# A hybrid decoder layer on one core: own buffers for the second recurrence's preparation, five weight-buffer pairs and a lag of two in the mixers, and the exclusive decay read as a shift

## The chip, the core and the metric

The kernel runs on one core of a Trainium2 chip. The metric is the device time of one execution in microseconds (us), lower is better. PE is the matrix engine (TensorE), DVE the vector engine, ACT the scalar engine, POOL is GpSimd, and SP issues most of the DMAs. The diff to be judged touches only the middle third of the program, and the memory pools around it.

## The reference, cut to what matters

A layer of width 2048 over 256 tokens, with three residual stages, all in float32:

```python
x = layer_norm(alpha * x + 0.5 * swiglu(x, ffn1...))             # d_ff 5632
p = x @ w_in                                                       # 3*1024 + 3*1024 + 288 columns
o_attn = diff_attn_group(p[..., :3072], ...)                       # 8 heads, causal
o_rwkv = rwkv7_group(p[..., 3072:], ...)                           # 16 heads of 64, a delta-rule recurrence
x = layer_norm(alpha * x + concat([o_attn, o_rwkv]) @ w_out)
x = layer_norm(alpha * x + 0.5 * swiglu(x, ffn2...))

# in rwkv7_group, per head and per token t (state is 64 x 64):
state = state * w_t + (state @ -kk_t) x (kk_t * a_t) + v_t x k_t   # w_t = decay, kk = normalised k
y_t   = state @ r_t
# afterwards: group norm of y, plus a bonus term, times a gate g
```

Inside a chunk of 64 tokens the kernel needs the running product of the decays up to and including a token (it multiplies r), and the product up to but *excluding* it (it multiplies kk). It keeps logarithms, so the first is exp of a running sum, and the second exp of that sum less the token's own term.

## The kernel before, in words

**Main matmuls.** Each weight matrix streams through SBUF in steps: SP loads two 128-row slices of 512 columns (`raw`, L127), ACT rounds them to `wh` (L130), and DVE subtracts to get the rest, `wl` (L131). Activations are split likewise into `xh` and `xl` (L80, L81). A product is three matmuls, hi*hi, lo*hi and hi*lo (L107, L108, L109), so a step is 12 main matmuls: 6 for token half tt=0 and 6 for tt=1. There are 664 steps and 7968 main matmuls. `stream.block` (L113) runs one block of 512 columns over its row slices. tt=1's half of a step is issued `LAG` = 4 steps behind tt=0's, and a ring of `NW` = 7 pairs `wh`, `wl` holds the weights.

**Program order.** All in-between work (recurrence, attention heads) is written as Python generators. After each step `run_bg` (L142) lets them write instructions up to a budget of credit. The engines then run their instructions in the order in which a list scheduler put them; every engine is a strict queue. The order is fixed before the run.

**The stages.** ffn1; LayerNorm 1 (L178 to L192); the mixers; LayerNorm 2 (the same lines); ffn2; LayerNorm 3. In the mixers the blocks of `w_in` come as: the 288-column lora block (8 steps), then k, r, v of recurrence group 1 (8 heads), v, k, q of attention group 1, and the same for group 2, 12 blocks of 8 steps (96 main matmuls). Then `w_out` runs in three parts of its rows: part (0,2) needs attention group 1 and recurrence group 1, part (1,) attention group 2, part (3,) recurrence group 2. Its partial sums stay in SBUF as `y` (written at L868, added to at L870).

**A recurrence group** (`rwkv_group`, L470). The *preparation*: lora matmuls and sigmoids (L485 to L490), running sum (L495), a subtract and three Exp (L497, L498, L500, L501), normalising kk (L507 to L521), products with the decays, the matrix `Q` of all chunks (L558, L561). Then a triangular *solve* as 62 short DVE operations (L581, L583) in a layout that a DMA makes and DMAs undo (L587, L588, L595, L599). Then the *chain*, the part that runs along the chunks (L606 to L680), and the group norm and gate (L693 to L728), which end in `og`, rows of `w_out`'s operand. Both groups use the same tiles `AR`, `BKc`, `vv`, `Q` and the scratch tiles T1, T2 and lw; group 2's generator is held until group 1's chain has been written (L472), and the writes of its r, k, v until group 1 has done with the tiles (L412, L420). All small products of both groups go through one PSUM pool, `sm`, with three banks, handed out in program order.

**The y buffers.** Of part (0,2)'s four column blocks two lie in tiles that the attention of group 2 still reads (`k` and an `H5` tile that holds v), so their L868 must wait for that.

## Time and profile before

| | us |
|---|---|
| runs | 2008.81, 2011.87, 2012.96; median 2011.87 |
| the profiled execution | 2011.4 |
| its span in the profile | 2009.6 |
| PE busy in the span | 1964.6 (98%) |
| PE's weight loads (PEld) | 1614.0 (80%) |
| DVE busy | 1148.2 (57%) |
| ACT busy | 888.1 (44%) |

The span runs from the first to the last instruction; the profiled execution's own time is 1.8 us longer. A row of the trace's timeline has a start, a duration, an engine, the line, the operation and its tiles, and in brackets how long the engine had been idle just before and who released it. Matmuls are pipelined, so durations of neighbours overlap: what one costs is the distance between starts. The granted clock (PEclk) is TensorE's clock as a share of 2.4 GHz.

### The profile page before, as it was taken

What the parts mean: (1) busy time and instruction counts of PE and PEld (TensorE: products, weight loads), DVE (VectorE), ACT (ScalarE), POOL (GpSimd) and SP (SyncE); (2) the same over time, 40 slices, a digit from 0 to 9 for tenths busy, and PEclk for the clock granted to TensorE, in tenths of its full rate; (3) what the DMA queues carried; (4) which work ended last, traced back from release to release, by engine and by line L of the source; (5) the groups of instructions that cost most, each with busy time, mean ns of one, the idle gap of its engine ahead of it and who ended that gap; (6) DMA issues with size and microseconds to landing.
All of it is one profiled execution on the core that took longest, in us unless ns stands there. A gap on an engine that the chain in (4) does not pass through costs nothing. (4 is left out here: it accounts for less than half of the span.)

```text
span 2009.6 us, 24928 instructions
## 1 busy us (share of the span) xinstructions
PE 1964.6 (98%) x9671; PEld 1614.0 (80%) x9671; DVE 1148.2 (57%) x1420; ACT 888.1 (44%) x1100; POOL 34.3 (2%) x68
## 2 busy tenths in 40 slices
PE   8999999999999999999999988999999999999997
PEld 7888888888888878887777767788888888888886
DVE  5555454445545566776667766745555444554555
ACT  5444443344444336645574444444444334444432
POOL 0200000000000000000000000000000000000000
PEclk9999999999999999999999979999999999999999
DMA  7766666667666656656535625666666666766663
GB/s 238 216 188 191 187 193 207 208 197 230 189 189 188 194 178 194 178 158 175 145 86 169 203 70 169 202 201 188 191 187 192 207 210 195 230 190 188 190 195 128
DMA packets 202008, 373.35 MB, mean 186 GB/s; under 512 B 22826, under 2 KB 24944, under 8 KB 201120
## 3 DMA queue, kind: packets, MB, share of 16 engines
q1 hardware_dynamic: 182928, 350.53, 58.2%
q10 hardware_dynamic: 17440, 14.29, 2.5%
q0 software_dynamic: 1520, 6.93, 1.1%
q8 instruction: 76, 1.25, 0.3%
q14 instruction: 44, 0.36, 0.1%
HBM read 364.10 MB, written 7.60 MB: 185 GB/s over the span
## 5 line engine op out<-in xcount | busy, mean ns | idle before, releaser
L131 DVE TENSOR_TENSOR wl<-raw,wh 128x1024 fp32r<-128x1024 f32 (+1 forms) x665 | 807.8, 1216 | 655.6 <-ACT wh L130 654.3
L130 ACT CAST wh<-raw 128x1024 fp32r<-128x1024 f32 (+1 forms) x665 | 695.8, 1047 | 840.6 <-PE acc L109 711.3
L109 PE MATMUL acc<-wh,xl 128*128 128x512 f32 (+1 forms) x1952 | 739.7, 390 | 1.5 <-DVE xl L81 1.5
L108 PE MATMUL acc<-wl,xh 128*128 128x512 f32 (+1 forms) x1952 | 736.3, 392 | 0.9 <-DVE wl L131 0.9
L107 PE MATMUL acc<-wh,xh 128*128 128x512 f32 (+1 forms) x1952 | 724.5, 391 | 9.4 <-ACT xh L80 7.5
L107 PEld LDWEIGHTS acc<-wh,xh 128*128 128x128 f32 x1952 | 367.4, 188 | 88.7 <-ACT xh L80 9.0
L108 PEld LDWEIGHTS acc<-wl,xh 128*128 128x128 f32 x1952 | 367.6, 188 | 77.0 <-issue 2.0
L109 PEld LDWEIGHTS acc<-wh,xl 128*128 128x128 f32 x1952 | 367.5, 188 | 75.9 <-DVE xl L81 2.0
L109 PE MATMUL acc<-wh,hh 128*128 128x512 f32 x704 | 254.4, 390 | 0.0
L108 PE MATMUL acc<-wl,hh 128*128 128x512 f32 x704 | 253.5, 389 | 0.0
L107 PE MATMUL acc<-wh,hh 128*128 128x512 f32 x704 | 252.7, 389 | 0.0
L108 PEld LDWEIGHTS acc<-wl,hh 128*128 128x128 f32 x704 | 132.2, 188 | 27.6
L109 PEld LDWEIGHTS acc<-wh,hh 128*128 128x128 f32 x704 | 132.2, 188 | 27.3
L107 PEld LDWEIGHTS acc<-wh,hh 128*128 128x128 f32 x704 | 132.1, 188 | 27.3
L234 DVE TENSOR_TENSOR hh<-tr,hh 128x512 fp32r<-128x512 f32 x44 | 30.4, 691 | 64.0 <-ACT hh L233 64.0
L233 ACT CAST hh<-tr 128x512 fp32r<-128x512 f32 x44 | 25.8, 587 | 91.0 <-PE tr L223 91.0
L220 DVE SCALAR_TENSOR_TENSOR h<-sg,acc 128x512 f32<-128x512 f32 x44 | 30.2, 687 | 34.9 <-PE acc L109 34.8
L215 ACT ACTIVATE sg<-acc 128x512 f32<-128x512 f32 x44 | 26.4, 600 | 43.6 <-PE acc L109 43.5
L581 DVE TENSOR_TENSOR itmp<-U,Y 64x31 f32<-64x31 f32 (+15 forms) x62 | 20.5, 331 | 11.5 <-DMA U<-dU 10.2
L223 PEld LDWEIGHTS tr<-ident,h 128*128 128x128 f32 x176 | 21.8, 139 | 5.7
L223 PE MATMUL tr<-ident,h 128*128 128x128 f32 x176 | 26.3, 271 | 0.0
L583 DVE TENSOR_TENSOR Y<-Y,itmp 64x31 f32<-64x31 f32 (+15 forms) x62 | 20.6, 332 | 1.4
(247 smaller groups left out, 750.8 us busy)
## 6 DMA issues: line engine op xcount, KB each, us to landing
raw<-in_ffn_w_up_dram SPq DMA_DIRECT2D x176, 512.0 KB, 3.9
raw<-in_ffn_w_down_dram SPq DMA_DIRECT2D x176, 512.0 KB, 4.2
raw<-in_ffn_w_gate_dram SPq DMA_DIRECT2D x175, 512.0 KB, 3.9
raw<-in_w_in_dram SPq DMA_DIRECT2D x96, 512.0 KB, 3.9
raw<-in_w_out_dram SPq DMA_DIRECT2D x32, 512.0 KB, 4.5
rc<-xs ACTq DMA_DIRECT2D x16, 256.0 KB, 4.3
lng<-in_ln_g_dram POOLq DMA_DIRECT2D x3, 1024.0 KB, 7.9
lnb<-in_ln_b_dram POOLq DMA_DIRECT2D x3, 1024.0 KB, 9.7
```

The costliest lines, as they stand in the source:

```text
L107: T.matmul(a, hi, wh[:, j, :w], start=(ki + j == 0), stop=False)
L108: T.matmul(a, hi, wl[:, j, :w], start=False, stop=False)
L109: T.matmul(a, lo, wh[:, j, :w], start=False, stop=(ki + j == last))
L130: SC.copy(out=wh[:, c, :w], in_=raw[:, c, :w])
L131: V.tensor_tensor(out=wl[:, c, :w], in0=raw[:, c, :w], in1=wh[:, c, :w].bitcast(F32), op=ALU.subtract)
L215: SC.activation(out=s, in_=acc, func=AF.Silu)
L220: V.scalar_tensor_tensor(out=h, in0=sg[tt], scalar=0.5, in1=acc, op0=ALU.mult, op1=ALU.mult)
L223: T.transpose(tr[:, i, :], h[:, i * P:(i + 1) * P], ident)
L233: SC.copy(out=hi, in_=tr)
L234: V.tensor_tensor(out=lo, in0=tr, in1=hi.bitcast(F32), op=ALU.subtract)
L581: V.tensor_tensor(out=tv, in0=U[:, 0:j, j:j + 1].to_broadcast([64, j, 32 - j]), in1=Y[:, j:j + 1, j:32].to_broadcast([64, j, 32 - j]), op= ...
L583: V.tensor_tensor(out=Y[:, 0:j, j:32], in0=Y[:, 0:j, j:32], in1=tv, op=ALU.add)
```

## The change

- **Buffers.** A class `Group` gives the second recurrence its own `AR`, `BK`, `vv` (tags ARd, BKd, vvd) and its own scratch (`tl`; `cum` lies in a half of `qq`). The two holds (L472 before, and the `until` calls in `done`) go; one hold is left, ahead of `Q`. The gate weights g2 no longer lie in `Q`.
- **Room for it.** In the mixers the ring has five pairs and the lag is two; in the two ffn stages seven and four as before. Two of the seven pairs lie in a pool of each stage.
- **Decay.** L497 and L498 go: the exclusive product at a token is the inclusive one of the token before it in the chunk, so `al[:, :, 1:64]` is multiplied by `cum[:, :, 0:63]`. The order of the preparation's products changes, and the first product of `be` and the copy `PC` move.
- **y and ln2.** `y` lies in group 1's old `AR` and `BK` memory (tags J0, BKc). LayerNorm 2's gain and bias, loaded by POOL, go to J1 and Q and are issued when part (3,) begins.
- **Credit.** Each generator has its own credit (`BG` 1.6, attention heads `AT` 0.5) in place of one shared budget.
- The scratch memory for DMA descriptors of GpSimd's queue is set to 2048.

```diff
-LAG = 4
-NW = 7
+LAG = {"ffn": 4, "mix": 2}
+NW = {"ffn": 7, "mix": 5}
...
-                wh = wp.tile([P, n, NB], F32R, tag="wh", name=nm("wh"), bufs=NW)
-                wl = wp.tile([P, n, NB], F32R, tag="wl", name=nm("wl"), bufs=NW)
+                pool = wp if self.slot < NW["mix"] else self.pool
+                wh, wl = (pool.tile([P, n, NB], F32R, tag=f"{t}{self.slot}", name=nm(t)) for t in ("wh", "wl"))
+                self.slot = (self.slot + 1) % NW[self.name]
...
-                if len(self.pend) > max(0, min(LAG, self.step // 4 - 1)):
+                if len(self.pend) > max(0, min(LAG[self.name], self.step // 4 - 1)):
...
-        AR = hp.tile([P, 4, 4, 2, 64], F32, tag="J0", name="AR")
-        BK = mp.tile([P, 4, 4, 3, 64], F32, tag="BKc", name="BKc")
-        vp = mp.tile([P, 4, 64 + S], F32, tag="vv", name="vv")
+        class Group:
+            def __init__(self, g):
+                self.AR = (hp, mp)[g].tile([P, 4, 4, 2, 64], F32, tag=("J0", "ARd")[g], name=nm("AR"))
+                self.BK = mp.tile([P, 4, 4, 3, 64], F32, tag=("BKc", "BKd")[g], name=nm("BK"))
+                self.vp = mp.tile([P, 4, 64 + S], F32, tag=("vv", "vvd")[g], name=nm("vv"))
...
-                    if prev is not None:
-                        stream.until(lambda: ("chain", "cols", "gate")[i] in prev)
...
-            prev = st["prev"]
-            while prev is not None and "chain" not in prev:
-                yield None
...
-            V.tensor_tensor(out=lw, in0=cum, in1=lw, op=ALU.subtract)
-            SC.activation(out=lw, in_=lw, func=AF.Exp, scale=-LDEC)
...
-            V.scalar_tensor_tensor(out=merge(al), in0=merge(al), scalar=-1.0, in1=merge(v4(lw)), op0=ALU.mult, op1=ALU.mult)
...
+            V.tensor_tensor(out=merge(al)[:, :, 1:64], in0=merge(al)[:, :, 1:64], in1=merge(v4(cum))[:, :, 0:63], op=ALU.mult)
...
-            while prev is not None and "end" not in prev:
+            while prev is not None and "chain" not in prev:
                 yield None
...
-        gb = load_gb(mp, A["ln2_g"], A["ln2_b"], "J0", "BKc")
+        gb = []
...
-                yt = [hp.tile([P, 2, NB], F32, tag="H3", name=nm("yt")), qq[:, 0].rearrange("p a s -> p (a s)").rearrange("p (t n) -> p t n", t=2),
-                      hp.tile([P, 2, NB], F32, tag=HT["k"], name=nm("yt"))]
-                yj = hp.tile([P, 2, NB], F32, tag="H5", name=nm("yv"))
+                yt = [hp.tile([P, 4, NB], F32, tag="J0", name=nm("y")), mp.tile([P, 4, NB], F32, tag="BKc", name=nm("y"))]
+                y = [[yt[n // 2][:, 2 * (n % 2) + t, :] for n in range(4)] for t in range(2)]
+            if 3 in qs:
+                gb.extend(load_gb(mp, A["ln2_g"], A["ln2_b"], "J1", "Q"))
...
-    nc = bacc.Bacc("TRN2", target_bir_lowering=False, num_devices=1)
+    nc = bacc.Bacc("TRN2", target_bir_lowering=False, num_devices=1, dynamic_dma_scratch_size=2048)
```

Where the instructions land, at three places. First, PE ahead of the second group's chain (acc is a main matmul's sum, YT the solve's transposed result, TT and PT blocks of the solve, ot an attention head's output). Before:

```order
4808 L108 MATMUL acc_9615<-wl_9667,xh_9144 128x512
4809 L109 MATMUL acc_9615<-wh_9666,xl_9145 128x512
4810 L109 MATMUL acc_9622<-wh_9586,xl_9149 128x512
4811 L107 MATMUL acc_9622<-wh_9586,xh_9148 128x512
4812 L108 MATMUL acc_9622<-wl_9587,xh_9148 128x512
4813 L109 MATMUL acc_9622<-wh_9586,xl_9149 128x512
4814 L606 MATMUL sm_8552<-YT_8548,Q 32x32 x32
4815 L617 MATMUL sm_8589<-TT_8542,PT_8549 32x32
4816 L627 MATMUL sm_8644<-ident,BKc 128x64 x8
4817 L825 MATMUL at_9343<-ident,ot_9279 128x128 x2
```

And now (lines have moved: L113 to L115 are the main matmuls, L608 was L606):

```order
4837 L115 MATMUL acc_9640<-wh_9629,xl_9150 128x512
4838 L113 MATMUL acc_9640<-wh_9668,xh_9149 128x512
4839 L114 MATMUL acc_9640<-wl_9669,xh_9149 128x512
4840 L115 MATMUL acc_9640<-wh_9668,xl_9150 128x512
4841 L113 MATMUL acc_9640<-wh_9668,xh_9149 128x512
4842 L114 MATMUL acc_9640<-wl_9669,xh_9149 128x512
4843 L608 MATMUL sm_8451<-YT_8447,Q 32x32 x32
4844 L115 MATMUL acc_9640<-wh_9668,xl_9150 128x512
4845 L619 MATMUL sm_8507<-TT_8441,PT_8448 32x32
4846 L629 MATMUL sm_8544<-ident,BK_7242 128x64 x8
4847 L829 MATMUL at_9414<-ident,ot_9319 128x128 x2
```

Counted over the whole order, 4542 main matmuls stand ahead of the first row of L606 before, and 4566 now: the 24 of part (0,2)'s last column block, tt=1, have moved ahead of the chain, and the first L825 of that head pair stood behind the chain's start and its counterpart now stands ahead of it.

Second, DVE where group 2's preparation starts (T, then qq, is the running sum; L708, L711, L713, later L711, L714, L716, finish group 1's norm). Before:

```order
696 L708 TENSOR_TENSOR BKc<-BKc,Q 128x16x64
697 L495 SCALAR_TENSOR_TENSOR T_1340_7273<-smask,lw_7252 128x256 x2
698 L711 TENSOR_SCALAR BKc<-BKc,vB 128x4x64 x4
699 L358 SCALAR_TENSOR_TENSOR AR<-praw_7845,om,df_7947 128x4x64
700 L524 TENSOR_SCALAR Q<-BKc,vB 128x256
701 L713 TENSOR_TENSOR Q<-BKc,vv 128x1024
702 L495 SCALAR_TENSOR_TENSOR T_1340_7273<-smask,lw_7252 128x256 x2
```

Now:

```order
692 L711 TENSOR_TENSOR BK_5614<-BK_5614 128x16x64
693 L714 TENSOR_SCALAR BK_5614<-BK_5614,vB 128x4x64 x4
694 L505 SCALAR_TENSOR_TENSOR qq<-smask,tl_7245 128x256
695 L138 TENSOR_TENSOR wl_8418<-raw_8416,wh_8417 128x1024
696 L716 TENSOR_TENSOR BK_5614<-BK_5614,vv_5615 128x16x64
697 L367 SCALAR_TENSOR_TENSOR AR_7241<-praw_7834,om,df_7923 128x4x64
698 L514 TENSOR_SCALAR BK_7242<-BK_7242,vB 128x4x64 x2
699 L505 SCALAR_TENSOR_TENSOR qq<-smask,tl_7245 128x256 x3
```

Group 2's running sum stands at the end of group 1's norm in both orders, beside the same weight step (the 352nd `wl`). It has not moved ahead of the first chain. Counted in main matmuls, group 2's lora product (L485, now L496) stands at 4117 before and 4129 now, its norm (L517, L519) at 4136 and 4175, and its `Q` (L558, L555) at 4237 to 4270 and 4257 to 4295; the solve begins beside `wl` 366 and 367 and ends beside `wl` 384 in both.

Third, ACT from the first LayerNorm 2 output to the first steps of ffn2 (at, sm: transposed columns; xs: the DMA that saves the normalised rows). Before:

```order
728 L192 DMA xs_83<-yt_9152 128x512
729 L80 CAST xh_10036<-at_10031 128x512
730 L192 DMA xs_83<-qq 128x512
731 L130 CAST wh_10231<-raw_10230 128x1024
732 L80 CAST xh_10048<-sm_10043 128x512
733 L192 DMA xs_83<-yt_9153 128x512
734 L80 CAST xh_10060<-at_10055 128x512
735 L130 CAST wh_10250<-raw_10249 128x1024
736 L192 DMA xs_83<-yv_9154 128x512
737 L80 CAST xh_10072<-sm_10067 128x512
738 L130 CAST wh_10268<-raw_10267 128x1024
```

Now:

```order
726 L201 DMA xs_83<-y_9154 128x512
727 L81 CAST xh_10073<-at_10068 128x512
728 L201 DMA xs_83<-y_9154 128x512
729 L81 CAST xh_10085<-sm_10080 128x512
730 L201 DMA xs_84<-y_9153 128x512 x2
731 L201 DMA xs_84<-y_9154 128x512 x2
732 L81 CAST xh_10126<-at_10121 128x512
733 L81 CAST xh_10138<-sm_10133 128x512
734 L81 CAST xh_10150<-at_10145 128x512
735 L81 CAST xh_10162<-sm_10157 128x512
736 L137 CAST wh_10248<-raw_10247 128x1024
737 L137 CAST wh_10266<-raw_10265 128x1024
```

The two casts of weights that stood between the first half's columns are gone from there: ffn2's sixth pair, `wh_10248`, has to wait for memory that the xs DMAs of the second half still read, and all four of those DMAs stand ahead of the second half's casts. In PE's order, 30 main matmuls of ffn2 now stand ahead of the second half's transposes, where about 44 stood; at the boundary from ffn1 to the mixers 30 of the 288-column matmuls, where 42 stood. Of `w_out`, 24 main matmuls follow the last one of the first token half (36 before), and 12 stand between the last transposes of part (1,) and the first that needs `og` (24 before).

## Rows read from the trace of the kernel before

**Rows 1.** The page: busy time by engine (its first part), and the chain that ended last, by engine.
```profile
PE 1964.6 (98%) x9671; PEld 1614.0 (80%) x9671; DVE 1148.2 (57%) x1420; ACT 888.1 (44%) x1100; POOL 34.3 (2%) x68
PE 37%; DVE 2%; ACT 1%; DMA 0%; issue 0%; DVEq 0%; ACTq 0%
```

**Rows 2.** Busy time by stretch: us from the span's start, length, then busy us (and instructions) of PE, PEld, DVE, ACT, POOL, the granted clock of PE, the DMA share, GB/s.
```profile
743.90:760.00 16.10, 12.64 (x93) 11.52 (x92) 15.61 (x27) 6.83 (x12) 0.99 (x1) 1.00 0.72 219
...
1040.00:1080.00 40.00, 37.91 (x201) 29.58 (x200) 33.38 (x43) 21.20 (x26) 0.00 (x0) 1.00 0.51 148
...
1150.00:1175.00 25.00, 17.52 (x245) 13.49 (x246) 14.48 (x39) 12.35 (x32) 2.01 (x2) 0.68 0.36 99
1175.00:1200.00 25.00, 21.70 (x259) 17.80 (x257) 17.99 (x56) 10.71 (x36) 2.01 (x2) 0.84 0.15 42
...
1250.00:1275.00 25.00, 21.52 (x101) 17.43 (x101) 24.86 (x38) 8.36 (x10) 2.00 (x2) 1.00 0.68 202
...
1300.00:1500.00 200.00, 200.00 (x902) 165.63 (x901) 102.11 (x92) 84.85 (x90) 0.30 (x2) 1.00 0.67 192
```

**Rows 3.** PE's timeline, main matmuls of 512 columns: the first and the last of thirteen in a row.
```profile
1146.05 0.39 PE L109 MATMUL acc<-wh,xl 128*128 128x512 f32 x1
...
1148.79 0.39 PE L109 MATMUL acc<-wh,xl 128*128 128x512 f32 x1
```

**Rows 4.** PE's timeline where ffn1 ends and the mixers' lora block begins: the first and the last of 39 matmuls of 288 columns in a row, and the second half's transposes that follow.
```profile
746.13 0.30 PE L107 MATMUL acc<-wh,xh 128*128 128x288 f32 x1
...
751.13 0.29 PE L109 MATMUL acc<-wh,xl 128*128 128x288 f32 x1
753.80 1.29 PE L74 MATMUL tr<-ident,y 128*128 128x128 f32 x8 [2.38 <-DVE y L187]
```

**Rows 5.** By source line: the subtract and the Exp of the exclusive decay (ns, minimum, median, maximum; first and last start).
```profile
L497 DVE TENSOR_TENSOR lw<-T,lw x2: 1217/1220/1224, 786.8 to 1036.2; 128x1024 f32<-128x1024 f32 x2
...
L498 ACT ACTIVATE lw<-lw x2: 1039/1043/1047, 789.5 to 1038.8; 128x1024 f32<-128x1024 f32 x2
```

**Rows 6.** Timelines of ACT and DVE in group 2's preparation: one table load, and DVE's longest wait there.
```profile
1040.78 1.28 ACT L520 ACT_TABLE_LOAD   x1
...
1027.15 1.23 DVE L708 TENSOR_TENSOR BKc<-BKc,Q 128x1024 f32<-128x1024 f32 x1 [5.83 <-ACT Q L706]
```

**Rows 7.** Timelines of DVE, ACT's DMA issues and PE from the end of group 2's solve to the start of its chain.
```profile
1144.73 0.18 DVE L583 TENSOR_TENSOR Y<-Y,itmp 64x31 f32<-64x31 f32 x1
1144.95 1.12 DVE L586 COPY U<-Y 64x1024 f32<-64x1024 f32 x1
...
1146.11 0.34 ACTq L588 DMA_DIRECT2D dYT<-U  x1
...
1152.49 0.98 ACTq L599 DMA_DIRECT2D YT<-dYT  x2
...
1152.22 0.40 PE L109 MATMUL acc<-wh,xl 128*128 128x512 f32 x1
1154.94 0.24 PE L606 MATMUL sm<-YT,Q 32*32 32x32 f32 x2 [2.32 <-DMA YT<-dYT]
```

**Rows 8.** Timelines of DVE and PE in the chain: the first and the last of three writes of y, and the first main matmul after the chain's first three quarters.
```profile
1172.52 0.67 DVE L868 SCALAR_TENSOR_TENSOR yt<-rc,acc 128x512 f32<-128x512 f32 x1
...
1186.08 0.68 DVE L868 SCALAR_TENSOR_TENSOR yv<-rc,acc 128x512 f32<-128x512 f32 x1
...
1192.94 0.50 PE L107 MATMUL acc<-wh,xh 128*128 128x512 f32 x1 [0.82 <-ACT xh L80]
```

**Rows 9.** Busy time by stretch again (columns as in Rows 2): the three stretches at the low clock, and the boundary to ffn2.
```profile
1155.80:1169.40 13.60, 11.30 (x182) 8.96 (x176) 8.70 (x23) 7.83 (x18) 1.01 (x1) 0.50 0.37 119
1172.80:1183.10 10.30, 8.39 (x92) 7.22 (x94) 7.29 (x25) 5.57 (x24) 0.00 (x0) 0.50 0.19 53
1227.50:1234.30 6.80, 3.46 (x8) 2.82 (x9) 3.86 (x6) 1.14 (x2) 0.54 (x1) 0.50 0.43 154
1259.80:1279.00 19.20, 14.86 (x78) 11.58 (x76) 19.17 (x29) 6.60 (x10) 1.00 (x1) 1.00 0.85 255
```

**Rows 10.** Timelines of PE and DVE from group 2's last norm product to the first matmul on `og`.
```profile
1217.80 1.89 PE L703 MATMUL sm<-Q,bones 128*128 128x256 f32 x8
...
1228.85 1.28 DVE L728 TENSOR_TENSOR og<-Q,sm 128x512 f32<-128x512 f32 x2
...
1230.84 0.80 PE L107 MATMUL acc<-wh,xh 128*128 128x512 f32 x1 [5.96 <-ACT xh L80]
```

**Rows 11.** Timelines of DVE and PE at LayerNorm 2: the last sum of the first half, the last cast of the second, and PE's last long waits.
```profile
1252.50 0.67 DVE L870 TENSOR_TENSOR yv<-yv,acc 128x512 f32<-128x512 f32 x1
...
1280.00 0.68 DVE L81 TENSOR_TENSOR xl<-sm,xh 128x512 fp32r<-128x512 f32 x1
...
1264.42 0.63 PE L74 MATMUL sm<-ident,yv 128*128 128x128 f32 x4 [1.73 <-DVE yv L187]
1266.12 0.50 PE L109 MATMUL acc<-wh,xl 128*128 128x512 f32 x1 [1.07 <-DVE xl L81]
```

**Rows 12.** DMA issues between 1250 and 1285 us: count, KB of one, median us from issue to landing.
```profile
xs<-yt ACTq DMA_DIRECT2D x4, 256.0 KB, 4.8
xs<-qq ACTq DMA_DIRECT2D x2, 256.0 KB, 3.7
```

**Rows 13.** The page's fifth part: all of DVE's weight subtractions (busy us, mean ns).
```profile
L131 DVE TENSOR_TENSOR wl<-raw,wh 128x1024 fp32r<-128x1024 f32 (+1 forms) x665 | 807.8, 1216 | 655.6 <-ACT wh L130 654.3
```

More of the change, by code (lines that the diff above doesn't have):

```diff
@@ L141, in flush, with spawn, run_bg @@
                 self.mm(self.pend.pop(0), 1)
-        def run_bg(self, budget):
-            self.credit = min(self.credit, 0.0) + budget
-            idle = 0
-            while self.bg and self.credit > 0 and idle < len(self.bg):
-                g = self.bg.pop(0)
-                try:
-                    cost = next(g)
-                except StopIteration:
-                    continue
-                self.bg.append(g)
-                if cost is None:
-                    idle += 1
-                else:
-                    idle = 0
-                    self.credit -= cost
+        def spawn(self, gen, rate):
+            self.bg.append(gen)
+            self.credit[gen] = [0.0, rate]
+        def run_bg(self):
+            for g in list(self.bg):
+                c = self.credit[g]
+                c[0] = min(c[0], 0.0) + c[1]
+                while c[0] > 0 and g in self.bg:
+                    try:
+                        cost = next(g)
+                    except StopIteration:
+                        self.bg.remove(g)
+                        break
+                    if cost is None:
+                        break
+                    c[0] -= cost
         def until(self, ready):
@@ L406, in rwkv_cols @@
             st["gen"] = rwkv_group(g, st)
-            stream.bg.append(st["gen"])
+            stream.spawn(st["gen"], BG)
             def done(tt, acc, i):
                 if tt == 0:
-                    if i == 2 and prev is not None:
-                        stream.until(lambda: "chain" in prev)
-                    pr = hp.tile([P, 4, S + 1], F32, tag=("H3", "H3", "J1")[i], name=nm("praw"))
+                    pr = hp.tile([P, 4, S + 1], F32, tag="J1" if g == 0 and i == 2 else "H3", name=nm("praw"))
                     V.memset(pr[:, :, 0:1], 0.0)
@@ L446, in rwkv_values @@
         def rwkv_values(g, st):
-            rk = st["rk"]
+            prev = st["prev"]
+            while "rk" not in st or (prev is not None and "chain" not in prev):
+                yield None
+            vp, vv, rk = st["group"].vp, st["group"].vv, st["rk"]
             SV = hp.tile([P, 4, 4, 2, 64], F32, tag="J1", name=nm("SV"))
@@ L521, in rwkv_group @@
[L521 to L526 removed]
+            SC.activation(out=tl, in_=tl, func=AF.Ln)
+            SC.activation(out=tl, in_=tl, func=AF.Exp, scale=-0.5)
@@ L562, in rwkv_group @@
                 yield 1.2
+            rk = t4("lw")
+            for p in range(4):
+                V.scalar_tensor_tensor(out=v4(rk)[:, p], in0=rh[:, p], scalar=col(4, g, p), in1=ka[:, p], op0=ALU.mult, op1=ALU.mult)
+            st["rk"] = rk
+            yield 1.5
             dU = dp.tile([64, 32, 32], F32, tag="dU", name=nm("dU"))
@@ L712, in rwkv_group @@
             yield 0.6
-            V.tensor_tensor(out=v4(sq), in0=Yc, in1=v4(vv), op=ALU.add)
+            V.tensor_tensor(out=sq, in0=Yc, in1=v4(vv), op=ALU.add)
             yield 0.6
             st["gate"] = True
-            while g == 0 and "r" not in st.get("next", ()):
+            while g == 0 and "v" not in st.get("next", ()):
                 yield None
-            o = (hp, mp)[g].tile([P, 4, S], F32, tag=("H3", "vv")[g], name=nm("og"))
+            o = (hp, mp)[g].tile([P, 4, S], F32, tag=("H3", "vvd")[g], name=nm("og"))
             for hf in range(2):
```

128 lines of the change are left out of this document (62 added, 66 removed).

## The prediction

> **What bounds the kernel now.** I read the page first. PE is busy for 1964.6 of 2009.6 us, and the chain that ended last runs over PE and hardly anything else [rows 1]. So the only time to be had is where PE stands idle or runs slowly, and a cheaper DVE or ACT instruction is worth nothing by itself. Next I read the busy time by stretch [rows 2]: in 200 us of ffn2 PE has no gap, and what it loses in the middle lies in a few places. Between ffn1 and the mixers it loses 16.1 - 12.6 = 3.5 us. In group 2's preparation (1040 to 1080) it loses 40.0 - 37.9 = 2.1 us. Around group 2's chain (1150 to 1200) it loses 10.8 us, and part of the rest runs at the low clock. It waits 6.0 us for og [rows 10], and at LayerNorm 2 it loses 19.2 - 14.9 = 4.3 us [rows 9]. That, with the slow matmuls inside, is all that this change can move.
>
> The unit for all that follows is one main matmul: thirteen starts in a row span 1148.79 - 1146.05 = 2.74 us, so 0.228 us each [rows 3]. One of 288 columns is 5.00 us / 38 = 0.132 us [rows 4].
>
> **The removed arithmetic.** Per group one DVE subtract of 1.22 us and one Exp of 1.04 us go [rows 5], and the orders hold three fewer table loads at 1.28 us each [rows 6]. For both groups this is 2.4 us of DVE and 2.1 + 3.8 = 5.9 us of ACT. The price on the path is zero, because PE's main matmuls cover both engines there; only in group 2's preparation, where PE lost 2.1 us and DVE once waited 5.8 us for ACT [rows 6], can it show. Bounds 0 and -2.1; I take -1.5, nearer to the end, since that stretch of ACT is where most of the removed work stood.
>
> **Own buffers.** The name of the change suggests that group 2 prepares itself during group 1's chain. The orders say that it doesn't: the running sum stands beside the same weight step, and lora product, norm and Q stand 12 to 39 matmuls later than before. The `sm` banks are handed out in program order, and that still puts group 2 behind group 1. I cost the earlier start at nothing. The solve ends beside the same weight step, so YT lands about when it did: the U copy ends at 1146.1, and PE saw YT at 1154.9, 8.9 us later [rows 7]. Bounds for its landing: 1153 (1.5 us less waiting in the preparation) and 1162 (the casts of the added matmuls' weights stand ahead of the transposing DMAs on ACT, and a ring of five could hold one up).
>
> **ffn1 to the mixers.** 12 fewer of the 288-column matmuls cover the second half's LayerNorm: 12 x 0.132 = 1.6 us. PE already waits 2.4 us there for DVE [rows 4], so uncovered work is lost in full, but DVE has two subtractions of 1.2 us fewer ahead of it [rows 13]. Bounds 0 and +1.6; I take +0.8, the middle. With the preparation, PE reaches the chain 0.7 us early by this.
>
> **The chain's start.** Before, PE ran out at 1152.2 (the last start) and waited for YT until 1154.94 [rows 7]. Now 24 more main matmuls stand in front: 24 x 0.228 = 5.5 us. PE gets to the chain at 1152.2 + 0.4 + 5.5 - 0.7 = 1157.4, later than YT's 1154.9, so this wait goes and the chain starts 2.5 us later than before. What is late next is the chain itself.
>
> **The chain.** It took 1192.94 - 1154.94 = 38.0 us until main matmuls resumed [rows 7, 8]. Three writes of y of 0.67 us stood in the middle of its DVE work [rows 8] and are now ahead of it: -2.0. The first head pair's last product no longer stands inside it, and the heads come earlier in the order: I take another -2.5. Upper bound: 38.0 (the chain's hand-overs between PE, DVE and ACT set it, and the writes only filled gaps); lower bound 30 (all of PE's 7.5 + 3.3 idle us at 1150 to 1200 [rows 2], less the 2.7 at its start, go). With 33.5, PE resumes at 1190.9, 2.1 us early.
>
> **og and w_out.** From the resumption to og it was 1230.84 - 1192.94 = 37.9 us [rows 8, 10]; the chain behind og is the same work on the same engines, and the lag has no part in it. I take 37.9 again, with bounds of 36 and 40 (a few us to either side, since PE's order beside it is new). PE has 12 fewer matmuls before og, so its wait grows from 6.0 to about 8.7 us, and 12 fewer after: -2.7. w_out then ends 2.1 + 2.7 = 4.8 us early, at 1255.2. The low clock after that wait (0.50 from 1227.5 to 1234.3 [rows 9]) lasts a little longer: +0.2.
>
> **LayerNorm 2 to ffn2.** Here the change takes cover away. DVE works without a gap from the last sum of the first half, 1252.5, to the second half's last cast, 1280.7 [rows 11]; in 1259.8 to 1279.0 it is busy 19.17 of 19.20 us [rows 9]. The lag of two puts that first sum 12 matmuls nearer to w_out's end, 2.7 us later, and five pairs take two weight subtractions out of the stretch, 2 x 1.216 = 2.4 us [rows 13]: DVE ends 0.3 us later, relative to w_out. Meanwhile PE has 14 main matmuls fewer (30 instead of about 44): 14 x 0.228 = 3.2 us. Two new waits come with it. All four xs transfers of the second half now stand ahead of the casts on ACT, which puts the first cast behind the fourth normalised column: bounds 0 and +1.5, I take +0.4, nearer to zero, because DVE's casts come behind those columns anyway. The sixth weight pair lies in memory that these transfers read; they land 3.7 to 4.8 us after issue [rows 12], so about 1283, and with a cast and a subtraction the pair is ready near 1285. PE has 30 matmuls of the second half until then, 6.8 us from 1279, to 1285.7: hidden, by under a us. I cost it at zero, and at +3 in the range. Sum for this boundary +3.9, bounds 0 and +8.
>
> The LayerNorm 2 gain and bias come later than before, on POOL; they are issued when part (3,) begins, so the wait for og, some 9 us, and w_out's last 108 matmuls, 25 us, cover them. The descriptor memory touches POOL's transfers alone. Both at zero.
>
> **The sum.** -4.8 + 0.2 + 3.9 = -0.7 us on the profiled 2011.4, which itself is 0.5 under the median of the runs: 2010.7 by the profile, 2011.2 against the median, and I say **2011**. A measurement of this kernel can tell about 0.2% from no change, 4 us.
>
> **The rule that speaks against it.** At the three places where PE had little to do, its clock was 0.50, which is 1.2 GHz, while at LayerNorm 2, with 4.3 us of gaps spread over 19, it stayed at 1.00 [rows 9]. In the wait for og and behind it, low clock and idleness together left PE 3.5 us of work in 6.8. Gaps of 8 us at LayerNorm 2 resemble the wait for og more than the present ones. The Trainium skill (TensorE: Matmul & The Clock Gate, section "HAM oscillation — how this bites in real kernels") describes such stalls: an array that idles between pieces of work is throttled and starts the next piece cold, so that a wait costs more than its length. By that rule the change would also lose clock at this boundary. The three low stretches agree with it; the boundary as it is now does not reach it.
>
> **Rivals.**
> *Slower, 2018.* The boundary to ffn2 goes cold. PE would be idle for some 7 us after w_out and 4 us before the second half, and if the clock drops after either, the matmuls behind it run at half speed over 7 to 14 us, as the two stretches around the chain did over 13.6 and 10.3 us [rows 9]. That is 3.5 to 7 us, say 4.5, and the sixth pair, no longer covered when its casts are late, adds 2.5: 2011 + 7 = 2018. It decides once the boundary costs 5 us more than the 3.9 I count. For it: DVE has no slack there and PE none to give. Against it: half-speed matmuls would also hide part of DVE's work, and PE has 30 matmuls to spread over the gap.
>
> *Faster, 2003.* The chain was held by the writes and head work mixed into it. If it takes 30 us instead of 33.5 (-3.5) and the boundary costs 1 instead of 3.9 (-2.9, the two subtractions and PE's own transposes filling it), and the preparation gives its whole 2.1 with no loss at the first boundary (-1.4), the time is 2011 - 7.8 = 2003. For it: 10.8 us of PE idle around the chain, with short hand-overs to DVE. Against it: the chain's own products depend on one another.
>
> *The change doesn't do what it says, 2011.* The preparation stays where it is (the orders say so), but the removed arithmetic and the y buffers are also hidden: the chain keeps 38.0 us (+4.5), the boundary costs only 1 (-2.9). This ends within 0.2% too, so it shares its sign with the forecast.
>
> **Chances.** Forecast 0.30, and the rival that ends in the same place 0.12: same 0.42. The faster case with all that ends under 2007.8: 0.31. The slower one with all over 2015.9: 0.27. The range: from 2003, the faster case, to 2019, the slower case with the third us of the sixth pair; what lies beyond is about 1 in 10 on either side.
>
> **What would show it.** In the profile after, the first chain product of group 2 (L608) should start near 1157 with no wait on a DMA ahead of it; main matmuls should resume near 1191; og's wait should be 8 to 9 us; w_out should end near 1255; and PE's idle time between w_out's end and the second half's first main matmul should be 8 us instead of 4.3. Wrong would be: a wait for YT that is still there (then the solve is later), a running sum of group 2 that comes before group 1's norm is done, L708 at 1027 [rows 6] (then the buffers do move it), or a granted clock of 0.50 behind w_out's end (then the slower rival holds).

## The result: slower, 2021.43 us, outside the range

| | us | ratio to before, 95% interval |
|---|---|---|
| before | 2012.17 (median of 11 runs) | |
| the change | 2021.43 (median of 11 runs, 2016.35 to 2024.89) | 1.0042 [1.0031, 1.0053] |
| the profiled execution of the change | 2024.08, span 2022.2 | |

The forecast was 2011, the range 2003 to 2019. The profiled executions differ by 12.7 us, more than the medians (9.3): the change's lies near the upper end of its eleven runs. Pieces of time below are those of one profiled execution each. By engine, the page of the change answers to [rows 1]:

```profile
PE 1977.3 (98%) x9671; PEld 1623.3 (80%) x9671; DVE 1147.5 (57%) x1419; ACT 883.7 (44%) x1095; POOL 35.7 (2%) x68
```

PE's idle time is the same as before, 44.9 us against 45.0; what has grown is its busy time, by 12.7, with as many instructions. That is a slower clock: the page gives a mean granted clock of 0.984 where it was 0.991. Leaving out the program's first 13 and last 10 us, PE spent 54.6 us at the low clock, where it had spent 30.7. By stretch (columns as in [rows 2]; the six long stretches, without two of 3.4 us):

```profile
751.10:757.90 6.80, 5.62 (x25) 5.42 (x26) 5.64 (x9) 2.61 (x5) 0.00 (x0) 0.50 0.43 154
1068.50:1075.30 6.80, 6.80 (x25) 5.58 (x22) 6.80 (x11) 2.09 (x2) 0.00 (x0) 0.50 0.70 231
1167.50:1177.70 10.20, 9.99 (x126) 8.39 (x126) 7.42 (x14) 6.67 (x10) 0.00 (x0) 0.50 0.51 168
1181.20:1191.40 10.20, 8.66 (x80) 7.46 (x81) 6.18 (x22) 5.13 (x21) 0.49 (x1) 0.50 0.01 2
1239.20:1246.00 6.80, 4.81 (x11) 3.80 (x12) 2.58 (x4) 2.13 (x3) 0.00 (x0) 0.50 0.00 0
1273.30:1280.10 6.80, 5.39 (x16) 3.76 (x16) 6.80 (x10) 2.26 (x4) 0.00 (x0) 0.50 1.04 328
```

The stretches around the chain and og stood there before [rows 9]. New against that execution are 751 (from ffn1 to the mixers), 1068 (group 2's preparation) and 1273 (LayerNorm 2). Each comes with a wait of PE. I took the lower clock for a consequence: something made PE wait in those places, or wait longer. For two of them that is only part of it, as other runs show (under LayerNorm 2 below).

The clock says how the time was lost, not why. For that I laid the starts of the same main matmuls of both traces side by side (counted from the first; times in us, of the profiled executions):

| piece of the path | before | forecast | measured |
|---|---|---|---|
| boundary ffn1 to mixers, how much later the 3217th matmul starts, relative to the 2185th | | +0.8 | +3.8 |
| start of group 2's chain | 1154.9 | 1157.4 | 1162.9 |
| chain, until main matmuls resume | 38.0 | 33.5 | 37.8 |
| from there to the first matmul on og | 37.9 | 37.9 | 40.5 |
| from there to w_out's last matmul | 28.7 | 26.2 | 26.6 |
| from there to the 5001st main matmul, in ffn2 | 55.3 | 59.2 | 59.3 |

The last two rows came out as worked, in their sums. The chain is where the forecast breaks: it starts 5.5 us later than I said, and is not shorter (4.3 us more than I said); the way to og adds 2.6. These three make up 12.4 of the 13.4 us by which this execution missed the forecast of 2010.7 for the profile. PE had no wait ahead of the chain; its timeline, and those of DVE and of ACT's issues, at the same places as [rows 7, 8]:

```profile
1151.95 1.13 DVE L588 COPY U<-Y 64x1024 f32<-64x1024 f32 x1
...
1153.11 0.34 ACTq L590 DMA_DIRECT2D dYT<-U  x1
...
1158.76 1.07 ACTq L601 DMA_DIRECT2D YT<-dYT  x2
...
1162.60 0.39 PE L114 MATMUL acc<-wl,xh 128*128 128x512 f32 x1
1162.91 1.20 PE L608 MATMUL sm<-YT,Q 32*32 32x32 f32 x64
```

The U copy, the solve's end, is at 1152.0, 7.0 us later than before, though it stands beside the same weight step in DVE's order. So the weight step itself is later. DVE's timelines at the 384th `wl`, before and in the change:

```profile
1142.61 1.23 DVE L131 TENSOR_TENSOR wl<-raw,wh 128x1024 fp32r<-128x1024 f32 x1 [0.57 <-ACT wh L130]
...
1148.63 1.21 DVE L138 TENSOR_TENSOR wl<-raw,wh 128x1024 fp32r<-128x1024 f32 x1
```

What delays the step, and what else delays the solve, the experiments had to tell.

### The profile page after: what moved, and what is told of

It reads as the page before. It is cut to its first block, busy times and chain, and to the rows that moved or that the text cites. A ratio compares the mean times of both kernels' runs of the same rounds, so it can differ in the third digit from the quotient of the medians.

```text
span 2022.2 us, 24923 instructions
## 1 busy us (share of the span) xinstructions
PE 1977.3 (98%) x9671; PEld 1623.3 (80%) x9671; DVE 1147.5 (57%) x1419; ACT 883.7 (44%) x1095; POOL 35.7 (2%) x68
## 5 line engine op out<-in xcount | busy, mean ns | idle before, releaser
L115 PE MATMUL acc<-wh,xl 128*128 128x512 f32 (+1 forms) x1952 | 741.8, 392 | 0.5 <-DVE xl L82 0.5
L113 PE MATMUL acc<-wh,xh 128*128 128x512 f32 (+1 forms) x1952 | 725.5, 392 | 8.5 <-ACT xh L81 5.6
L113 PEld LDWEIGHTS acc<-wh,xh 128*128 128x128 f32 x1952 | 368.9, 189 | 87.5 <-ACT xh L81 7.1
L115 PEld LDWEIGHTS acc<-wh,xl 128*128 128x128 f32 x1952 | 368.9, 189 | 77.2 <-issue 2.0
L115 PE MATMUL acc<-wh,hh 128*128 128x512 f32 x704 | 254.4, 390 | 0.0
L113 PE MATMUL acc<-wh,hh 128*128 128x512 f32 x704 | 252.8, 389 | 0.0
L113 PEld LDWEIGHTS acc<-wh,hh 128*128 128x128 f32 x704 | 132.1, 188 | 27.4
L115 PEld LDWEIGHTS acc<-wh,hh 128*128 128x128 f32 x704 | 132.2, 188 | 27.3
L583 DVE TENSOR_TENSOR itmp<-U,Y 64x31 f32<-64x31 f32 (+15 forms) x62 | 20.6, 333 | 4.1 <-DMA U<-dU 2.8
L585 DVE TENSOR_TENSOR Y<-Y,itmp 64x31 f32<-64x31 f32 (+15 forms) x62 | 20.6, 332 | 1.3
```

The source lines that it names most:

```text
L113: T.matmul(a, hi, wh[:, j, :w], start=(ki + j == 0), stop=False)
L115: T.matmul(a, lo, wh[:, j, :w], start=False, stop=(ki + j == last))
L583: V.tensor_tensor(out=tv, in0=U[:, 0:j, j:j + 1].to_broadcast([64, j, 32 - j]), in1=Y[:, j:j + 1, j:32].to_broadcast([64, j, 32 - j]), op= ...
L585: V.tensor_tensor(out=Y[:, 0:j, j:32], in0=Y[:, 0:j, j:32], in1=tv, op=ALU.add)
```

## The experiments

The ratios below are to the kernel before, timed again with each group of runs (medians 2012.77, 2012.00 and 2013.24 us). Differences in us are taken from 2012.17 and 2021.43, so one us either way says nothing.

I began with two theories. **Theory 1**: the lost cover (five pairs, lag two) makes PE wait at the boundaries, and the clock falls there. **Theory 2**: the separate credits and buffers put the chain's end later in the order. A first group of four runs was made for these.

**e1, the ring and the lag alone.** Mixers with five pairs and lag two, on the kernel before:

```diff
-LAG = 4
-NW = 7
+LAG = {"ffn": 4, "mix": 2}
+NW = {"ffn": 7, "mix": 5}
...
-                wh = wp.tile([P, n, NB], F32R, tag="wh", name=nm("wh"), bufs=NW)
-                wl = wp.tile([P, n, NB], F32R, tag="wl", name=nm("wl"), bufs=NW)
+                wh, wl = (wp.tile([P, n, NB], F32R, tag=f"{t}{self.slot}", name=nm(t)) for t in ("wh", "wl"))
+                self.slot = (self.slot + 1) % NW[self.name]
...
-                if len(self.pend) > max(0, min(LAG, self.step // 4 - 1)):
+                if len(self.pend) > max(0, min(LAG[self.name], self.step // 4 - 1)):
```

Expected: 

> The kernel before with five weight pairs and a lag of two in the mixers and nothing else of the change (the other two pairs stay allocated and idle there). Theory 1 (the lost cover): the two LayerNorm boundaries and the wait for og lose their cover and TensorE drops to 0.50 behind them, so this alone costs 7 to 10 us over before, with low-clock stretches near 751 and behind w_out's end. Theory 2 (the order): group 2's chain and og are written later by the separate credits and the own buffers, and the ring matters little: 0 to 4 us over before.

Measured: 2003.37 us, ratio 0.9957 [0.9942, 0.9971]. It is *faster* than before by 8.8 us, where both theories had it slower or equal. The boundaries do cost what theory 1 says: from w_out's last matmul to the 5001st it takes 59.4 us, much as in the change, and at 751 to 757 the clock is 0.50. But group 2's solve ends at 1132.1 instead of 1145.0, and that gives more than it costs. The reason, as I read the code, is that a lag of two delivers every block's second half two steps earlier to what waits for it; no run takes that apart. The 384th `wl` starts at 1149.1 here, as late as in the change: with five pairs a weight step comes later on the clock. The solve ends early because it ends beside an earlier step, the 379th.

**e2, the lag alone**, with seven pairs:

```diff
-LAG = 4
+LAG = {"ffn": 4, "mix": 2}
...
-                if len(self.pend) > max(0, min(LAG, self.step // 4 - 1)):
+                if len(self.pend) > max(0, min(LAG[self.name], self.step // 4 - 1)):
```

Expected: 

> The kernel before with a lag of two in the mixers, but all seven weight pairs. Theory 1: with seven pairs 42 to 44 matmuls of the next stage still stand ahead of the second half's transposes, so the boundary from ffn1 costs nothing and the one to ffn2 about half: +1 to +4 us over before. Theory 2: 0 to +4, from the later place of og in PE's order.

Measured: 2005.93 us, ratio 0.9967 [0.9958, 0.9977]. The boundary from ffn1 costs nothing here (the 3301st main matmul starts at 771.0, 772.2 before and 775.4 in e1), and the one to ffn2 3.2 us (58.5 instead of 55.3). So the first boundary's loss goes with the ring, and the second's mostly with the lag. The solve ends at 1136.3, and the 384th `wl` starts at 1138.3: the late weight step goes with the ring as well. (The profiled execution, 2010.05 us, is the slowest of e2's ten.)

**e3, the shift alone**, on the kernel before:

```diff
-            V.tensor_tensor(out=lw, in0=cum, in1=lw, op=ALU.subtract)
-            SC.activation(out=lw, in_=lw, func=AF.Exp, scale=-LDEC)
...
-            V.scalar_tensor_tensor(out=merge(al), in0=merge(al), scalar=-1.0, in1=merge(v4(lw)), op0=ALU.mult, op1=ALU.mult)
+            V.tensor_tensor(out=merge(al)[:, :, 1:64], in0=merge(al)[:, :, 1:64], in1=merge(v4(cum))[:, :, 0:63], op=ALU.mult)
```

Expected: 

> The kernel before with only the exclusive decay read as a shift (one DVE subtract and one Exp per group gone, and a table load where they force one). Both theories: within 2 us of before. A gain of 4 us or more would say that the removed arithmetic is worth something by itself and that the rest of the change costs more than its 9 us.

Measured: 2001.53 us, ratio 0.9942 [0.9923, 0.9962]: 10.6 us for some 4 us of arithmetic per group. As said beforehand, it means that the rest of the change costs more than 9 us. The U copy and the chain's first product in its timeline, against 1144.95 and 1154.94 before [rows 7]:

```profile
1135.82 1.12 DVE L584 COPY U<-Y 64x1024 f32<-64x1024 f32 x1
...
1147.90 1.20 PE L604 MATMUL sm<-YT,Q 32*32 32x32 f32 x64
```

The solve ends 9.1 us earlier, and PE does not run dry ahead of the chain, nor inside it: before, no main matmul started between 1152.2 and 1192.9 [rows 7, 8], and here they go on at 1149.0.

**e4, the change with the shared credit:**

```diff
-            for g in list(self.bg):
-                c = self.credit[g]
-                c[0] = min(c[0], 0.0) + c[1]
...
+            self.credit = min(self.credit, 0.0) + budget
+            idle = 0
+            while self.bg and self.credit > 0 and idle < len(self.bg):
+                g = self.bg.pop(0)
...
-                self.run_bg()
+                self.run_bg(BG)
```

Expected: 

> The changed kernel with the one shared credit of 1.6 per step of the kernel before in place of a credit for each generator. In PE's order group 2's norm moves from main matmul 4689 back to 4651 and its gate product from 4692 to 4674. Theory 1: within 2 us of the changed kernel (+7 to +10 over before). Theory 2: 4 to 7 us faster than the changed kernel, that is +2 to +5 over before, with the first matmul on og 4 to 7 us earlier.

Measured: 2014.82 us, ratio 1.0009 [0.9998, 1.0019]; 6.6 us less than the change. Theory 2 has its share: the solve ends at 1150.7, hardly earlier, but the first matmul on og comes at 1233.7 instead of 1241.2. It leaves the larger part open. Ring and lag alone and the shift alone each gain, and still the change is 11 and 13 us behind them with the credits undone: something in the rest costs at least that.

So I looked again at the changed preparation, at the tiles that it writes. DVE and ACT before, in group 2's preparation (the square, the two norm sums, the Ln, kk times its norm, the first entries of Q):

```profile
1008.24 1.06 ACT L511 ACTIVATE Q<-AR 128x1024 f32<-128x1024 f32 x1 [0.91 <-PE sm L673]
...
1037.82 1.28 DVE L518 TENSOR_SCALAR Q<-sm 128x512 f32<-128x512 f32 x2
...
1042.07 1.06 ACT L520 ACTIVATE Q<-Q 128x1024 f32<-128x1024 f32 x1
...
1045.54 1.23 DVE L528 TENSOR_TENSOR AR<-AR,Q 128x1024 f32<-128x1024 f32 x1 [3.69 <-ACT Q L521]
...
1069.32 1.88 DVE L561 TENSOR_TENSOR Q<-sm,maskq 128x512 f32<-128x512 f32 x3
```

And in the change:

```profile
1041.91 1.06 ACT L512 ACTIVATE tl<-AR 128x1024 f32<-128x1024 f32 x1 [0.90 <-DVE qq L505]
...
1048.17 0.68 DVE L520 TENSOR_SCALAR tl<-sm 128x512 f32<-128x512 f32 x1
...
1051.10 1.06 ACT L522 ACTIVATE tl<-tl 128x1024 f32<-128x1024 f32 x1
...
1055.91 1.23 DVE L526 TENSOR_TENSOR AR<-AR,tl 128x1024 f32<-128x1024 f32 x1 [1.16 <-ACT tl L523]
...
1057.60 1.05 ACT L529 ACTIVATE tl<-qq 128x1024 f32<-128x1024 f32 x1
...
1072.07 1.88 DVE L558 TENSOR_TENSOR Q<-sm,maskq 128x512 f32<-128x512 f32 x3
```

Before, the square of kk lay in a slice of Q and was taken at 1008: k was there by 1004, and the row shows the last wait, for a product of group 1's chain (L673), which reads Q. Now it is written to `tl`, the tile in which the sigmoids lie until the running sum has read them, so it waits for that sum (released by DVE L505) until 1041.9. The inverse decay goes to `tl` as well and waits in turn for the product with the norm. This is **theory 3**: the change gives each group buffers of its own, but inside a group one scratch tile does the work of three, and what ran side by side runs in a row. **Theory 4**: the separate credits and y's place are the cost, and the scratch is not. A second group of four:

**e5, the change with its scratch apart:**

```diff
+            sq, pinv = (Qt[:, i * 1024:(i + 1) * 1024].rearrange("p (a s) -> p a s", a=4) for i in (1, 2))
-            SC.activation(out=v4(tl), in_=al, func=AF.Square)
+            SC.activation(out=v4(sq), in_=al, func=AF.Square)
...
-            SC.activation(out=tl, in_=cum, func=AF.Exp, scale=LDEC)
+            SC.activation(out=pinv, in_=cum, func=AF.Exp, scale=LDEC)
```

(and `sq`, `pinv` for `tl` wherever the two are read).

Expected: 

> The changed kernel, but the squares and norms of kk, and the inverse decay, lie in slices of Q (free until Q is written) instead of in tl, which the sigmoids and the running sum use too. Theory 3 (one scratch tile for five things): in the change the Square must wait for the running sum, and the inverse decay for the product with the norm, so the preparation runs as one chain; with the tiles apart, group 2's norm stands at main matmul 4149 to 4170 in PE's order instead of 4217, Q at 4262 to 4296 instead of 4299 to 4337, and the time falls by 8 to 14 us against the changed kernel, to 2007 to 2013. Theory 4 (the separate credits and y's place are the cost, the scratch is not): within 3 us of the changed kernel.

Measured: 2001.21 us, ratio 0.9947 [0.9932, 0.9962]: 20 us less than the change, more than expected.

**e6, the scratch apart and the shared credit** (the edits of e4 and e5 together).

Expected: 

> The changed kernel with both: scratch tiles apart as in the run before, and the shared credit of 1.6. Theory 3: the two add up only in part, since the chain's end can be late only once: 2001 to 2009. Theory 4: as the changed kernel with shared credit, 2013 to 2017.

Measured: 1997.78 us, ratio 0.9930 [0.9913, 0.9947]. The separate credits cost 3.4 us here (four runs of each, which don't overlap). This beats both kernels, and every part tried so far.

**e7, one scratch tile in the kernel with the shift.** The converse: on e3, sigmoids, squares, norms and the inverse decay all in T2; the two Exp of the running sum and the copy `PC` move behind the product with the norm, as in the change.

```diff
-            lw = t4("lw")
+            lw = t4("T2")
...
-            sq = tmp4[1]
+            sq = lw
...
-            pinv = t4("T2")
+            pinv = lw
```

Expected: 

> The kernel before with the decay as a shift, and with one scratch tile (T2) for sigmoids, squares, norms and inverse decay, as in the change; ring, lag, credit and the other buffers are those of before. Theory 3: slower than the shift alone (2001.5) by 4 to 10 us, the chain starting later by about 11 matmuls or more. Theory 4: within 2 us of the shift alone.

Measured: 2010.44 us, ratio 0.9992 [0.9982, 1.0001]: 8.9 us slower than the shift alone, and nearly the whole gain of the shift is gone. The square again waits for the running sum, and the wait for YT is back. Its timelines of ACT, DVE and PE:

```profile
1036.45 1.06 ACT L503 ACTIVATE T<-AR 128x1024 f32<-128x1024 f32 x1 [1.00 <-DVE T L495]
...
1051.56 1.23 DVE L520 TENSOR_TENSOR AR<-AR,T 128x1024 f32<-128x1024 f32 x1 [3.73 <-ACT T L513]
...
1143.62 1.13 DVE L583 COPY U<-Y 64x1024 f32<-64x1024 f32 x1
...
1154.15 0.24 PE L603 MATMUL sm<-YT,Q 32*32 32x32 f32 x2 [2.29 <-DMA YT<-dYT]
```

**e8, shift, ring and lag on the kernel before** (the edits of e1 and e3).

Expected: 

> The kernel before with the shift, five pairs and a lag of two: the parts that were measured as gains, without own buffers, separate credits, and y and LayerNorm 2's weights moved. If the two gains add up in full, 1992; if both come from the same place (an earlier end of group 2's solve), 1997 to 2003. If the change's own scratch and credits are its whole cost, the changed kernel with both undone comes out near this one.

Measured: 2002.65 us, ratio 0.9961 [0.9946, 0.9976]. The gains of e1 and e3 don't add up. The time lies in the range said for one common place, but the trace doesn't show that they share one: the solve ends earlier than in either (1129.5), and the chain starts at 1141.4, 6.5 us before e3's. It is lost behind that: from the chain's start to w_out's last matmul it takes 109.8 us, where e3 has 100.6 and e1 104.5, and both boundaries cost what they cost in e1. Why that stretch is longer stays open; the profiled execution, 2006.77 us, is also the slowest of the four. And e6 is 4.9 us better than this; what is left in e6 beside these parts are the own buffers, the new order of the preparation's products, y's place and LayerNorm 2's late weights, of which I tried none alone.

A third group asked which of the two uses of the scratch it was, and what the credits cost by themselves.

**e9, only squares and norms apart** (e5's edits for `sq`, without those for `pinv`).

Expected: 

> The changed kernel with only the squares and norms of kk in a slice of Q of their own; the inverse decay stays in tl behind the running sum. If the Square that waits for the running sum is the cost (theory 3a), this alone gives what both did: 1999 to 2004, group 2's solve ending near 1126 instead of 1152. If it is the inverse decay that waits for the product with the norm (theory 3b): 2013 or more.

Measured: 1999.51 us, ratio 0.9934 [0.9919, 0.9949]. Alone it gives what both did. DVE's and PE's timelines:

```profile
1037.15 1.28 DVE L521 TENSOR_SCALAR Q<-sm 128x512 f32<-128x512 f32 x2
...
1044.10 1.23 DVE L527 TENSOR_TENSOR AR<-AR,Q 128x1024 f32<-128x1024 f32 x1 [1.89 <-ACT Q L524]
...
1060.70 1.88 DVE L559 TENSOR_TENSOR Q<-sm,maskq 128x512 f32<-128x512 f32 x3
...
1125.11 1.07 DVE L589 COPY U<-Y 64x1024 f32<-64x1024 f32 x1
...
1137.28 0.24 PE L609 MATMUL sm<-YT,Q 32*32 32x32 f32 x2
```

The solve ends 26.8 us earlier than in the change, and the chain begins 25.6 us earlier, while PE still has main matmuls to put between its steps: when the chain starts, 4523 of them have started in e9, 4607 in the change (4584 before, 4568 in e3). The clock from 1150 to 1175 in the change, and in e9:

```profile
1150.00:1175.00 25.00, 21.83 (x220) 17.72 (x220) 17.25 (x41) 11.86 (x24) 3.42 (x2) 0.85 0.71 196
...
1150.00:1175.00 25.00, 22.10 (x195) 16.79 (x194) 19.27 (x39) 12.05 (x28) 1.01 (x1) 1.00 0.53 170
```

The earlier start goes through to the end: from the chain's start to w_out's last matmul it takes 104.0 us in e9, 104.9 in the change and 104.6 before.

**e10, only the inverse decay apart** (e5's edits for `pinv`).

Expected: 

> The changed kernel with only the inverse decay in a slice of Q of its own; squares and norms stay in tl behind the running sum. Theory 3a: part of the gain, since the norm stands at main matmul 4195 in PE's order (4217 in the change, 4149 to 4170 with the norm apart): 2007 to 2015. Theory 3b: 1999 to 2004.

Measured: 2007.05 us, ratio 0.9977 [0.9967, 0.9986]: part of the gain, 14 us against the change. The square still waits for the running sum; the solve ends at 1139.8. So the two uses don't add up: with the inverse decay apart, taking the square out as well gives another 6 us (e5), and with the square apart, the inverse decay is worth nothing (e9).

**e11, the separate credits alone**, on the kernel before.

Expected: 

> The kernel before with a credit for each generator (1.6, attention heads 0.5), nothing else. If the separate credits cost by themselves what undoing them gave in the change (6.6 us) and in the change with the scratch apart (3.4 us): 2015 to 2019. If they cost only where the chain ends late, with five pairs and a lag of two: within 2 us of before.

Measured: 2012.15 us, ratio 0.9992 [0.9982, 1.0002]: no cost by itself. What the credits cost in the change (6.6 us) and beside the scratch apart (3.4) hangs on the other parts; why there and not here I did not settle.

## Why the prediction was wrong

**The step that failed is "own buffers", where I wrote that the solve ends beside the same weight step, "so YT lands about when it did".** It does end beside the same step, the 384th, but 7.0 us later, and the DMAs that bring YT are issued 6.3 us later (1158.8, before 1152.5). The step failed in two ways. A weight step is no clock when the ring changes: with five pairs the 384th comes at 1148.6 to 1149.7 in the change, e1 and e9, with seven at 1142.6 before and 1138.3 in e2. And the same step was not the best to be had: e1 ends its solve beside the 379th, e9 beside the 377th. What kept the change from an earlier step is its one scratch tile. I should have asked which tiles the new preparation writes. I counted what the own buffers free, and read from the orders that the preparation does not start earlier, but not that it had become one chain inside each group. The order had it in plain sight: norm 39 matmuls and Q 20 to 25 later than before, though two instructions a group had gone. I noted the rows and costed them at nothing, because PE had work beside them. What was lost there is 22 us (e9 against the change).

**Two gains were missing as well.** The removed arithmetic I bounded by PE's idle time in 1040 to 1080, 2.1 us; the shift alone gives 10.6 us (e3). The bound was the wrong kind: in this stretch PE's idle time does not measure what an earlier preparation is worth, for PE is kept busy there by matmuls that it lacks later, inside the chain. And the lag stood in my sum only as lost cover; e2, the lag alone, is 6 us faster than before. Without the loss in the scratch the change would have been 13 us faster than before (e9), so a forecast near no change had too little on both sides.

How a delay in the preparation becomes 27 us I read from the solve. Both groups have the one tile, and part of the delay comes from group 1: its norm products start at 1010.9 in e9 and 1018.2 in the change. Group 2's own norm products are then 13.0 us apart (1031.0, 1044.0), and its solve begins 16.4 us later. I summed DVE's durations between the solve's first addition and the U copy, in the profiled executions:

| kernel | solve begins | ends | length | its own work | weight subtractions | other work | median time |
|---|---|---|---|---|---|---|---|
| e9 | 1079.2 | 1125.1 | 46.0 | 20.4 | 17.1 (14) | 7.6 | 1999.5 |
| e3 | 1085.0 | 1135.8 | 50.8 | 20.3 | 19.4 (16) | 13.2 | 2001.5 |
| before | 1089.7 | 1145.0 | 55.3 | 20.3 | 21.8 (18) | 14.2 | 2012.2 |
| the change | 1095.6 | 1152.0 | 56.3 | 20.4 | 20.6 (17) | 16.2 | 2021.4 |

Neighbouring rows overlap a little, so the three can add up to more than the length. DVE's busy time says how full it is: 91 to 94% in the four, so it has little to spare. The solve in e9 and in the change (columns as in [rows 2], DVE is the third):

```profile
1079.20:1125.10 45.90, 45.90 (x217) 37.04 (x217) 42.14 (x88) 24.60 (x40) 0.96 (x1) 1.00 0.53 167
...
1095.60:1152.00 56.40, 56.40 (x265) 45.28 (x264) 51.44 (x117) 28.67 (x55) 1.34 (x2) 1.00 0.57 183
```

A solve that begins 16 us later meets more weight subtractions, five writes of y in place of one, and more of group 2's attention heads, and its 62 short operations queue behind them. It then ends 27 us later, for the same own work. Only then come the transposing DMAs and the chain. The solve's end goes with the time across the runs, though not alone: e1, e2 and e8 end it at 1132.1, 1136.3 and 1129.5 and pay some of it back at the boundaries, e8 also behind the chain.

Point by point, for the rest.

*The chain's start*: PE no longer waits for YT there, as forecast, but only because it was itself late by 5.5 us (1162.9, not 1157.4).

*The chain*: 37.8 us, my upper bound and not the 33.5. I had taken three writes of y out of it; one is still inside (1169.4) and one right ahead of its first product (1162.6). Some 23 us of it ran at 0.50 (24 before), and at 1167.70 PE had waited 3.2 us while DVE's copy of PT, at 1166.9, stood behind two weight subtractions and a wait for POOL.

*og*: 2.6 us longer than I took it, and the order showed that too; PE's wait for it was 5.0 us, not 8.7. Group 2's norm products after the chain stand 41 matmuls later in the order (4689 against 4648; counted in the traces, where all positions are some 42 higher than in my counts ahead of the prediction, with the same differences), so they sat behind main matmuls; with the shared credit they stand at 4651 and og comes 7.5 us earlier (e4). The credits alone don't set that place: e10, with separate ones, has 4651 too, and e2, with the shared one, 4692.

*ffn1 to the mixers*: 3.8, not 0.8. The wait ahead of the second half's transposes grew from 2.4 us [rows 4] to 3.4, and from inside it on the clock was 0.50 for 6.8 us, while it had held before. Not all of this is the change's: in e3 and e11, with ring and lag as before, the clock fell there too, for 3.4 us, and the piece took 1.6 us more than in the execution before. PE's timelines in the change, in e3, and in e2, where the clock held:

```profile
752.28 1.94 PE L75 MATMUL tr<-ident,y 128*128 128x128 f32 x8 [3.43 <-DVE y L196]
...
751.18 1.36 PE L74 MATMUL tr<-ident,y 128*128 128x128 f32 x8 [2.53 <-DVE y L187]
...
752.60 1.29 PE L74 MATMUL tr<-ident,y 128*128 128x128 f32 x8 [2.54 <-DVE y L193]
```

*LayerNorm 2*: 4.0 where I had worked 3.9, but by another way. From w_out's end to the second half's first main matmul PE was idle for 5.1 us, not 8 (4.3 before); the rest of the loss is matmuls at the low clock, the rival's, which I had named as a sign of being wrong. That the sum came out was luck. PE's timeline, and its busy time over the boundary:

```profile
1271.54 0.66 PE L75 MATMUL at<-ident,y 128*128 128x128 f32 x4 [3.33 <-DVE y L196]
...
1273.99 1.11 PE L75 MATMUL at<-ident,y 128*128 128x128 f32 x4 [0.63 <-DVE y L196]
...
1276.98 0.80 PE L114 MATMUL acc<-wl,xh 128*128 128x512 f32 x1 [0.55 <-DVE wl L138]
...
1287.74 0.50 PE L113 MATMUL acc<-wh,xh 128*128 128x512 f32 x1 [0.33 <-ACT xh L81]
...
1267.80:1287.70 19.90, 14.78 (x64) 10.60 (x62) 18.87 (x28) 5.78 (x9) 1.00 (x1) 0.83 0.66 196
```

The slower rival named the place, and PE did go cold there; but the boundary's whole loss is 4.0 us, where the rival's own sum made it 10.9, so it was right in its sign for the wrong reason. Nor does the low clock need the lost cover: in e3 and e11, with the waits of before within 0.1 us, it fell at this boundary too, for 6.8 us, and the piece took 56.7 and 56.6 us instead of 55.3. PE's waits before, and in e3:

```profile
1264.42 0.63 PE L74 MATMUL sm<-ident,yv 128*128 128x128 f32 x4 [1.73 <-DVE yv L187]
1266.12 0.50 PE L109 MATMUL acc<-wh,xl 128*128 128x512 f32 x1 [1.07 <-DVE xl L81]
...
1253.36 0.63 PE L74 MATMUL sm<-ident,yv 128*128 128x128 f32 x4 [1.79 <-DVE yv L187]
1255.06 0.80 PE L109 MATMUL acc<-wh,xl 128*128 128x512 f32 x1 [1.07 <-DVE xl L81]
```

The rule of the Trainium skill that I set beside it (TensorE: Matmul & The Clock Gate, section "HAM oscillation — how this bites in real kernels") agrees with what the change's trace shows at both boundaries: idle time of 3.4 and 3.3 us, and low clock with and behind it. It does not tell e3 from e2 at the first boundary, nor e3 from the kernel before at the second.

## What to carry to other kernels

Where a change hands a stage its own buffers, list for each tile everything that is written to it, and who must have read it by then: a scratch tile that takes three roles turns parallel work into a chain, and a list scheduler follows that faithfully. An engine that stays busy in a stretch does not show that the stretch's other work is free; ask where the bound engine next runs dry, and trace back from there. A place in an order is not a time: compare it only between kernels whose other stream runs as far ahead. Where a long train of small operations shares a nearly full engine, a late start can grow: here 16 us became 27.

## What the runs showed of the hardware that I had not expected

TensorE's clock fell to 0.50 in a wait of 3.4 us for the second half's columns, with dense matmuls right ahead of the wait and behind it (751 to 758), where in the kernel before it had stayed at 1.00 around one of 2.4 us [rows 2, 4]. But the length of the wait does not decide it here: of three runs with waits of 2.53, 2.54 and 2.60 us at that place, two fell for 3.4 us (e3, e11) and one stayed (e2). At LayerNorm 2 the waits of before (0.67, 1.73 and 1.07 us) and those of e3 (0.68, 1.79 and 1.07) are alike, and only e3 fell. So a boundary like this one can be cold in one kernel and warm in another without a change to it, and 1 to 2 us of difference there, in one execution each, are no evidence for a change.

And the whole 12.7 us between the two profiled executions appears as busy time of PE, with 23.9 us more at the low clock and idle time unchanged: a comparison of idle times alone would have shown no difference at all.
